# A second seven-product group in every other gate-and-up pair, and silu in one ScalarE pass

## The chip, the cores and the metric

The kernel runs on one core of one Trainium2 chip, in one launch. The metric is the device time of that launch in microseconds, as the median of several runs.

## The reference, cut to what matters

Two layers over 256 tokens of width 2048. Each has a gated mixer (convolution and attention), a SwiGLU feed-forward block with 5632 hidden columns, and an embedding stage. Everything is float32. The part that the change touches is the feed-forward block and the norm ahead of it:

```python
hf = rmsnorm(x, norm_ffn_g[i])
gate, up = jnp.split(hf @ w_gate_up[i], 2, axis=-1)
x = x + (jax.nn.silu(gate) * up) @ w_down[i]
```

## The kernel before, in words

**Splits.** TensorE multiplies in a rounded 32-bit format (`fp32r`). To keep float32's accuracy each operand is split into a high and a low half, and a product is three matmuls: high x high, high x low, low x high (`Sum.add`, lines 175 to 177). A weight tile of 128 x 1024 (two row tiles of 128 by 512 columns; "raw") is fetched by one DMA on SyncE's queue (`fetch`, L134), ScalarE writes its high half `wh` (L140), and VectorE subtracts to get the low half `wl` (L141). There are seven `raw` buffers, and four each of `wh` and `wl`. Activations are split once, when a norm or an `operand` is made, and stay in `pair` buffers, of which there are 23.

**Chunks.** A weight matrix is cut into chunks of 512 output columns. A chunk of w_gate_up has 16 row tiles ("column tiles" of the activation), in four groups of four. In the plain form (`plain`) one raw takes part in 12 matmuls of 128 x 512: two row tiles, two blocks of 128 tokens, three matmuls each.

**The seven-product form.** `fast_chunks` computes two chunks together (w1 and w2; in the feed-forward block a gate chunk and the up chunk that belongs to it). For one group of four row tiles the activation is seen as a 2 x 2 block matrix and the weights as another, and the eight block products are replaced by seven (Winograd's form of Strassen's scheme), named p1, q5, q7, q6, c21, c11 and c12 after the sums that they go to. Each product is six matmuls. The weight sums that it needs are made from the four raws a11, a21, a22, a12 with four 1024-wide adds on VectorE (L242; one of them goes to a buffer `s3`, called "sum" in the profile, the others are in place), and each of the seven operands is split like a raw. Sums p1, q5, q6, q7 stand in the four `ms` banks of PSUM and are combined (L255 on ScalarE; L256, L257 and two L242 on VectorE) as soon as q6 is done. c11, c12, c21, c22 stand in the four `mm` banks; into them go also all plain halves of the other groups. `go` takes the next such half from the list `left`: it fetches, splits and multiplies it, and unless it is called quietly it lets one waiting piece of other work run (`run`). Such pieces are the "turns": transposing the result of the pair before and splitting it into the operand of the next matrix.

**Activations for that form.** An object of `Fast` keeps the blocks of four column tiles and four differences of them (L325), split into high and low halves (L334 on ScalarE, L335 on VectorE). `Norm` makes one such object for its column tiles 0 to 3; the others are split plainly (`halves`, L287 and L288 with the norm's gain, L284 and L285 without). `operand` does the same for the hidden tiles: the first chunk of each part gives a `Fast`, the others plain tiles.

**The feed-forward block.** The 11 pairs c = 0 to 10 run in three parts of 3, 4 and 4. After each part its hidden chunks are multiplied with w_down, two output chunks at a time. Pair c = 0 is computed plainly; all others go through `fast_chunks` with `norm.fast` and the groups that begin at tiles 4, 8 and 12 in the plain form. When the gate chunk is complete, `gate` is called: a Sigmoid with the norm's scale on ScalarE (L868) and a scalar-tensor-tensor on VectorE (L869) give silu; when the up chunk is complete, L877 multiplies.

The order of instructions on each engine is made by the framework's scheduler when the kernel is built: it follows the program's order by priority, but can put an instruction ahead of others when its inputs and a buffer are there. Buffers of a pool are handed out as they come free.

Of the kernel before, what the change touches and what calls it, by code (L numbers as in the profile page):

```python
# [10 lines left out]
F32 = mybir.dt.float32  # L11
# [5 lines left out]
P = 128  # L17
# [27 lines left out]
def trunk(ctx, tc, xT, xR, pT, wI, wF, wC, wA, wOut, wGU, wD, wPG, wPP, vec, bF, gF, out):  # L45
# [86 lines left out]
    def fetch(src):  # L132
        raw = raws.tile([P, 2, 512], F32, tag="raw", name=f"raw{next(uid)}")
        nc.sync.dma_start(raw.rearrange("p k n -> p (k n)"), src)  # L134
        return raw

    def split(raw):
        h = whs.tile([P, 2, 512], F32R, tag="wh", name=f"wh{next(uid)}")
        l = wls.tile([P, 2, 512], F32R, tag="wl", name=f"wl{next(uid)}")
        act.activation(h, raw, AF.Copy)  # L140
        dve.tensor_tensor(l, raw, h.bitcast(F32), op=ALU.subtract)  # L141
        return h, l
# [68 lines left out]
    def fast_chunks(fast, w1, w2, xs, ks, first, to=None):  # L211

        nk = 4 * len(ks)
        p1, q5, q6, q7 = (Sum(2, bank_ms) for _ in range(4))
        c11, c12, c21 = (Sum(2 + nk, bank_mm) for _ in range(3))
        c22 = Sum(nk, bank_mm)
        left = deque()
        for w, sums in ((w1, (c11, c12)), (w2, (c21, c22))):  # L220
            for g, k0 in enumerate(ks):
                for half in range(2):
                    left.append((w[1 + g][:, half * 1024 : (half + 1) * 1024], sums, k0 + 2 * half))

        def go(n=1, quiet=False):
            for _ in range(n):
                if left:
                    src, sums, k0 = left.popleft()
                    parts = split(fetch(src))
                    await_x(xs, (k0, k0 + 1))  # L230
                    plain(sums, xs, k0, parts)
                    fill(CONV // 2 + len(left) % 2)
                    if not quiet:
                        run()

        def product(to, which, raw):
            h, l = split(raw)
            xh, xl = fast(which)
            for kk in range(2):
                to.add(xh(kk), xl(kk), h[:, kk, :], l[:, kk, :])  # L240

        add = lambda o, a, b: dve.tensor_tensor(o, a, b, op=ALU.add)  # L242
        a11, a21 = fetch(w1[0][:, :1024]), fetch(w2[0][:, :1024])
        a22, a12 = fetch(w2[0][:, 1024:]), fetch(w1[0][:, 1024:])
        s3 = raws.tile([P, 2, 512], F32, tag="raw", name=f"sum{next(uid)}")
        product(p1, B11, a11)
        add(s3, a11, a21)
        add(a21, a21, a22)
        product(q5, M1, a21)
        go(quiet=True)  # L250
        product(q7, T3, s3)
        add(a11, a11, a21)
        product(q6, T2, a11)
        u1, u4, u3, u5 = [tmp() for _ in range(4)] if to is None else to
        act.activation(u1, p1.t, AF.Copy)  # L255
        dve.tensor_tensor(u4, u1, q6.t, op=ALU.subtract)  # L256
        dve.tensor_tensor(u3, u4, q7.t, op=ALU.add)  # L257
        add(u4, u4, q5.t)
        add(u5, u3, q5.t)
        go()  # L260
        product(c21, N4X, a22)
        go()
        product(c11, B21, a12)
        go()
        add(a12, a12, a11)
        product(c12, B22, a12)
        while len(left) > 2 * len(ks):
            go()
        add(u1, u1, c11.t)
        add(u4, u4, c12.t)  # L270
        first((u1, u4))
        go(2 * len(ks))
        dve.tensor_tensor(u3, c21.t, u3, op=ALU.subtract)
        dve.tensor_tensor(u5, c22.t, u5, op=ALU.subtract)
        return u3, u5
# [94 lines left out]
    class Norm:  # L370


        def __init__(self, gcol, fast=False):
            self.gcol, self.xs, self.tiles = gcol, {}, {}
            self.fast = Fast() if fast else None
            self.ss = small(8)

        def gain(self, k):
# [8 lines left out]

        def turn(self, n):
            for half, pt in turned(lambda b: xt[:, b, n * 512 : (n + 1) * 512]):
                if n == 0 and self.fast:  # L390
                    self.fast.take(half, pt, [self.gain(2 * half + kk) for kk in range(2)])
                    if half == 1:
                        self.xs.update(enumerate(self.fast.column_tiles()))
                    continue
                o = pair(F32R)
                for kk in range(2):
                    k = 4 * n + 2 * half + kk
                    halves(o[:, kk, :], pt[:, kk, :], self.gain(k))
                    self.tiles[k] = o[:, kk, :]
                    self.xs[k] = by_blocks(self.tiles[k])  # L400
# [62 lines left out]
        take(0)  # L463

    def early():
        norm.fast = Fast()
        for j in range(2):
            norm.fast.take(
                j, xin[0][:, j, :].rearrange("p (k s) -> p k s", k=2), [norm.gain(2 * j + kk) for kk in range(2)]
            )  # L470
        norm.xs.update(enumerate(norm.fast.column_tiles()))

    def rest(q):
        def go():
# [15 lines left out]
    for i in range(L):  # L490
# [71 lines left out]
        def logits():  # L562
            pf = bank_ms()
            lhsT = lambda k: wfc[:, k].rearrange("p a h -> p (a h)")
            for k in range(4, KD):
                pe.matmul(pf[:16, :], lhsT=lhsT(k), rhs=norm.tiles[k], start=(k == 4), stop=False)
            for k, (hi, lo) in enumerate(norm.fast.both()):
# [272 lines left out]
                xc = xt[:, b, n * 512 : (n + 1) * 512]  # L840
                dve.tensor_tensor(xc, xc, acc[b], op=ALU.add)  # L841

        norm = Norm(g_ffn, fast=True)
        def onto_x(norm, n):
            def go(y):
                residual(n, y)
# [3 lines left out]

        for n in range(0, N4, 2):
            onto_x(norm, n + 1)(
                fast_chunks(fast_merged, wOut[i, n], wOut[i, n + 1], merged, (4, 8, 12), onto_x(norm, n))
            )


        after = Norm(g_ple, fast=True)
        c0 = 0
        for part, nch in enumerate(FFN_PARTS):
            hid = {}  # L860
            fast_hid = Fast()
            for c in range(c0, c0 + nch):
                w1, w2 = wGU[i, 2 * c], wGU[i, 2 * c + 1]
                z = [tmp() for _ in range(2)]

                def gate(g, z=z):
                    for b in range(2):
                        act.activation(z[b], g[b], AF.Sigmoid, scale=norm.r(b))  # L868
                        dve.scalar_tensor_tensor(z[b], g[b], norm.r(b), z[b], op0=ALU.mult, op1=ALU.mult)  # L869

                if c == 0:
                    gate(chunk(by_four(w1), norm.xs, bank_mm))
                    up = chunk(by_four(w2), norm.xs, bank_mm)
                else:
                    up = fast_chunks(norm.fast, w1, w2, norm.xs, (4, 8, 12), gate)
                for b in range(2):
                    dve.scalar_tensor_tensor(z[b], up[b], norm.r(b), z[b], op0=ALU.mult, op1=ALU.mult)  # L877
                o = z
                turns.append(
                    lambda c=c, o=o, hid=hid, fast=fast_hid if c == c0 else None:  # L880
                    operand(hid, 4 * c, lambda b: o[b], fast)
                )
            for n in range(0, N4, 2):
                await_x(hid, (4 * c0,))
                on = after if part == len(FFN_PARTS) - 1 else None
                onto_x(on, n + 1)(
                    fast_chunks(
                        fast_hid, wD[i, n][c0 : c0 + nch], wD[i, n + 1][c0 : c0 + nch], hid,
                        range(4 * c0 + 4, 4 * c0 + 4 * nch, 4), onto_x(on, n),
                    )  # L890
                )
# [16 lines left out]
        after = Norm(0 if last else (i + 1) * NV, fast=not last)  # L908
        e = []

        def embedded(n):
# [93 lines left out]
```

## Time and profile before

| what | value |
|---|---|
| median of 3 runs | 2848.05 us (2847.43 to 2848.83) |
| the profiled execution's own time | 2847.62 us |
| its span, first to last instruction | 2845.8 us |
| TensorE busy | 2815.2 us, 99% |
| VectorE busy | 2366.3 us, 83% |
| ScalarE busy | 1556.2 us, 55% |
| mean granted TensorE clock | 0.997 |
| moved by DMA | 543.27 MB, 191 GB/s |

In the profile's rows PE is TensorE, PEld its weight loads, DVE VectorE, ACT ScalarE, SP SyncE, and SPq its DMA queue. A row of a group gives line, engine, operation, output <- inputs, shapes and count; then the busy time in us, the mean of one in ns, and behind the last bar the idle time of the engine just before them with what ended it. A row of a timeline gives start and duration in us, and in square brackets the idle time before it; "x2" means that two in a row are shown as one. A row of the view by stretches gives, for each engine, busy time and instructions in that stretch. A busy TensorE is not one at its peak, since neighbouring matmuls overlap in the rows.

### The profile page before, as it was taken

To read this page: it belongs to the slowest core of one execution; us is meant where nothing else is said; L and a number is where in the kernel's file an instruction comes from. 1 tells how busy PE (TensorE), PEld (TensorE's weight loads), DVE (VectorE), ACT (ScalarE), POOL (GpSimd) and SP (SyncE) were. 2 spreads that over 40 slices of the span, in tenths; PEclk is the share of its full clock that TensorE was granted. 3 is DMA by queue.
4 is the path that set the end of the run, shared out by engine and by line. 5 is a ranking of instruction groups with operands and counts; after the bars stand their busy time and mean duration, and the time that the engine had idled before them with its cause. 6 is when DMAs were issued, how large, how long until landed. Compare 5 with 4: busy or idle time off the path is not lost.

```text
span 2845.8 us, 34651 instructions
## 1 busy us (share of the span) xinstructions
PE 2815.2 (99%) x12724; PEld 2328.0 (82%) x12724; DVE 2366.3 (83%) x3032; ACT 1556.2 (55%) x1874; POOL 9.5 (0%) x40
## 2 busy tenths in 40 slices
PE   8999999999999999999999999999999999999997
PEld 6888888888888888888788888888888888888886
DVE  6998877878888888888869988778688888888886
ACT  6445755555555545556644466455555555455564
POOL 0000000000000000000000000000000000000000
PEclk9999999999999999999999999999999999999999
DMA  7554465565556566555555545555555556556563
GB/s 283 177 179 170 161 205 191 175 205 182 190 199 207 186 203 207 185 193 193 195 174 191 180 155 186 199 192 174 196 193 195 197 196 210 186 195 210 178 217 125
DMA packets 149497, 543.27 MB, mean 191 GB/s; under 512 B 16848, under 2 KB 17104, under 8 KB 149072
## 3 DMA queue, kind: packets, MB, share of 16 engines
q1 hardware_dynamic: 149328, 541.07, 56.0%
q8 instruction: 99, 1.62, 0.2%
q14 instruction: 70, 0.57, 0.1%
HBM read 538.91 MB, written 2.10 MB: 190 GB/s over the span
## 4 chain that ended last, share of the span: by engine, by line
PE 92%; DVE 6%; ACT 1%; issue 1%; DMA 1%; SPq 0%; ACTq 0%; POOLq 0%; POOL 0%; DVEq 0%
PE mm L177 27%; PE mm L176 26%; PE mm L175 26%; PE ms L175 3%; PE ms L177 3%; PE ms L176 3%; DVE wl L141 2%; DVE pair L514 2%; PE ms L297 2%; DMA pair<-in_xT_dram 0%; PE ms L674 0%; ACT wh L140 0%; DVE raw L242 0%; PE ms L710 0%; DMA raw<-in_wI_dram 0%
## 5 line engine op out<-in xcount | busy, mean ns | idle before, releaser
L140 ACT ACTIVATE wh<-raw 128x1024 fp32r<-128x1024 f32 x1110 | 1177.7, 1062 | 1126.2 <-PE mm L177 923.6
L141 DVE TENSOR_TENSOR wl<-raw,wh 128x1024 fp32r<-128x1024 f32 x1110 | 1345.7, 1223 | 424.6 <-ACT wh L140 410.8
L175 PE MATMUL mm<-wh,pair 128*128 128x512 f32 x3552 | 1392.5, 392 | 12.4 <-ACT wh L159 7.5
L176 PE MATMUL mm<-wl,pair 128*128 128x512 f32 x3552 | 1385.6, 390 | 0.5 <-DVE wl L141 0.4
L177 PE MATMUL mm<-wh,pair 128*128 128x512 f32 x3552 | 1385.2, 390 | 0.8 <-DVE pair L285 0.8
L175 PEld LDWEIGHTS mm<-wh,pair 128*128 128x128 f32 x3552 | 667.9, 188 | 148.9 <-ACT wh L159 7.5
L177 PEld LDWEIGHTS mm<-wh,pair 128*128 128x128 f32 x3552 | 667.6, 188 | 141.3 <-DVE pair L285 1.7
L176 PEld LDWEIGHTS mm<-wl,pair 128*128 128x128 f32 x3552 | 668.3, 188 | 138.1 <-DVE wl L141 2.0
L514 DVE SCALAR_TENSOR_TENSOR pair<-pair,vecs,pair 128x256 f32<-128x256 f32 x480 | 203.8, 489 | 0.0
L242 DVE TENSOR_TENSOR raw<-raw,raw 128x1024 f32<-128x1024 f32 x144 | 175.9, 1221 | 1.8
L175 PE MATMUL ms<-wh,pair 128*128 128x512 f32 x416 | 162.9, 392 | 2.1 <-ACT pair L932 2.1
L177 PE MATMUL ms<-wh,pair 128*128 128x512 f32 x416 | 161.9, 389 | 0.0
L176 PE MATMUL ms<-wl,pair 128*128 128x512 f32 x416 | 161.9, 389 | 0.0
L175 PEld LDWEIGHTS ms<-wh,pair 128*128 128x128 f32 x416 | 78.1, 188 | 19.2 <-ACT pair L932 3.2
L177 PEld LDWEIGHTS ms<-wh,pair 128*128 128x128 f32 x416 | 78.1, 188 | 16.3
L176 PEld LDWEIGHTS ms<-wl,pair 128*128 128x128 f32 x416 | 78.1, 188 | 16.0
L140 ACT ACTIVATE wh<-sum 128x1024 fp32r<-128x1024 f32 x48 | 51.0, 1063 | 65.4 <-PE mm L177 65.4
L141 DVE TENSOR_TENSOR wl<-sum,wh 128x1024 fp32r<-128x1024 f32 x48 | 58.6, 1221 | 11.6 <-ACT wh L140 11.6
L242 DVE TENSOR_TENSOR sum<-raw,raw 128x1024 f32<-128x1024 f32 x48 | 58.6, 1221 | 1.5 <-DMA raw<-in_wGU_dram 0.9
L841 DVE TENSOR_TENSOR xt<-xt,tmp 128x512 f32<-128x512 f32 x80 | 51.8, 684 | 0.0
L242 DVE TENSOR_TENSOR tmp<-tmp,mm 128x512 f32<-128x512 f32 x80 | 51.5, 681 | 0.0
L242 DVE TENSOR_TENSOR tmp<-tmp,ms 128x512 f32<-128x512 f32 x80 | 51.2, 681 | 0.0
(176 smaller groups left out, 1142.8 us busy)
## 6 DMA issues: line engine op xcount, KB each, us to landing
raw<-in_wGU_dram SPq DMA_DIRECT2D x352, 512.0 KB, 4.3
raw<-in_wI_dram SPq DMA_DIRECT2D x287, 512.0 KB, 4.0
raw<-in_wD_dram SPq DMA_DIRECT2D x176, 512.0 KB, 4.0
raw<-in_wOut_dram SPq DMA_DIRECT2D x64, 512.0 KB, 3.9
raw<-in_wPG_dram SPq DMA_DIRECT2D x64, 512.0 KB, 4.2
raw<-in_wA_dram SPq DMA_DIRECT2D x32, 512.0 KB, 4.6
raw<-in_wC_dram SPq DMA_DIRECT2D x32, 512.0 KB, 4.7
raw<-in_wPP_dram SPq DMA_DIRECT2D x8, 512.0 KB, 5.1
```

What stands on the lines that cost most here:

```text
L140: act.activation(h, raw, AF.Copy)
L141: dve.tensor_tensor(l, raw, h.bitcast(F32), op=ALU.subtract)
L175: pe.matmul(self.t, lhsT=xh, rhs=wh, start=start, stop=False)
L176: pe.matmul(self.t, lhsT=xh, rhs=wl, start=False, stop=False)
L177: pe.matmul(self.t, lhsT=xl, rhs=wh, start=False, stop=self.left == 0)
L242: add = lambda o, a, b: dve.tensor_tensor(o, a, b, op=ALU.add)
L297: pe.transpose(pt[:, kk * S + b * P : kk * S + (b + 1) * P], src(b)[:, c : c + P], ident)
L514: dve.scalar_tensor_tensor(cv[c], u[c][:, j : j + S], w, cv[c], op0=ALU.mult, op1=ALU.add,)
L841: dve.tensor_tensor(xc, xc, acc[b], op=ALU.add)
```

## The change

`fast_chunks` takes a list of `Fast` objects and does one seven-product group for each. `Norm` can make several; the norm ahead of the feed-forward block now makes two, for column tiles 0 to 3 and 4 to 7. Pairs with odd c (1, 3, 5, 7, 9) use both, and have the groups at 8 and 12 left in the plain form; pairs with even c keep one. With two groups, p1, q5, q6, q7 gather both before they are combined, and `run` is held back until then (`state["quiet"]`). `gate` is a single Silu with the norm's scale on ScalarE. All other callers pass one object.

```diff
-        p1, q5, q6, q7 = (Sum(2, bank_ms) for _ in range(4))
-        c11, c12, c21 = (Sum(2 + nk, bank_mm) for _ in range(3))
+        p1, q5, q6, q7 = (Sum(nf, bank_ms) for _ in range(4))
+        c11, c12, c21 = (Sum(nf + nk, bank_mm) for _ in range(3))
...
+        for g, f in enumerate(fast):
+            a11, a21 = fetch(w1[g][:, :1024]), fetch(w2[g][:, :1024])
+            a22, a12 = fetch(w2[g][:, 1024:]), fetch(w1[g][:, 1024:])
+            s3 = raws.tile([P, 2, 512], F32, tag="raw", name=f"sum{next(uid)}")
+            product(p1, f(B11), a11)
+            add(s3, a11, a21)
+            add(a21, a21, a22)
+            product(q5, f(M1), a21)
             go()
+            product(q7, f(T3), s3)
+            add(a11, a11, a21)
+            product(q6, f(T2), a11)
+            if g == len(fast) - 1:
+                act.activation(u1, p1.t, AF.Copy)
+                dve.tensor_tensor(u4, u1, q6.t, op=ALU.subtract)
+                dve.tensor_tensor(u3, u4, q7.t, op=ALU.add)
+                add(u4, u4, q5.t)
+                add(u5, u3, q5.t)
+                state["quiet"] = False
+                go()
+            product(c21, f(N4X), a22)
+            if len(left) > 2 * len(ks):
+                go()
+            product(c11, f(B21), a12)
+            if g == 0 and len(left) > 2 * len(ks):
+                go()
+            add(a12, a12, a11)
+            product(c12, f(B22), a12)
+        go(len(left) - 2 * len(ks))
...
-            self.fast = Fast() if fast else None
+            self.fast = [Fast() for _ in range(fast)]
...
-                if n == 0 and self.fast:
-                    self.fast.take(half, pt, [self.gain(2 * half + kk) for kk in range(2)])
+                if n < len(self.fast):
+                    self.fast[n].take(half, pt, [self.gain(4 * n + 2 * half + kk) for kk in range(2)])
...
-        norm = Norm(g_ffn, fast=True)
+        norm = Norm(g_ffn, fast=2)
...
-                        act.activation(z[b], g[b], AF.Sigmoid, scale=norm.r(b))
-                        dve.scalar_tensor_tensor(z[b], g[b], norm.r(b), z[b], op0=ALU.mult, op1=ALU.mult)
+                        act.activation(z[b], g[b], AF.Silu, scale=norm.r(b))
...
-                    up = fast_chunks(norm.fast, w1, w2, norm.xs, (4, 8, 12), gate)
+                    nf = 1 + c % 2
+                    up = fast_chunks(norm.fast[:nf], w1, w2, norm.xs, (4, 8, 12)[nf - 1 :], gate)
```

More of the change, by code (lines that the diff above doesn't have):

```diff
@@ L211, in fast_chunks @@
     def fast_chunks(fast, w1, w2, xs, ks, first, to=None):
-        nk = 4 * len(ks)
-        p1, q5, q6, q7 = (Sum(2, bank_ms) for _ in range(4))
-        c11, c12, c21 = (Sum(2 + nk, bank_mm) for _ in range(3))
+        nf, nk = 2 * len(fast), 4 * len(ks)
+        p1, q5, q6, q7 = (Sum(nf, bank_ms) for _ in range(4))
+        c11, c12, c21 = (Sum(nf + nk, bank_mm) for _ in range(3))
         c22 = Sum(nk, bank_mm)
@@ L222, in fast_chunks, with go, product @@
                 for half in range(2):
-                    left.append((w[1 + g][:, half * 1024 : (half + 1) * 1024], sums, k0 + 2 * half))
-        def go(n=1, quiet=False):
+                    left.append((w[len(fast) + g][:, half * 1024 : (half + 1) * 1024], sums, k0 + 2 * half))
+        state = dict(quiet=True)
+        def go(n=1):
             for _ in range(n):
[L227 to L236, printed above, removed]
+                src, sums, k0 = left.popleft()
+                parts = split(fetch(src))
+                await_x(xs, (k0, k0 + 1))
+                plain(sums, xs, k0, parts)
+                fill(CONV // 2 + len(left) % 2)
+                if not state["quiet"]:
+                    run()
+        def product(to, operand, raw):
             h, l = split(raw)
-            xh, xl = fast(which)
+            xh, xl = operand
             for kk in range(2):
@@ L242, in fast_chunks @@
         add = lambda o, a, b: dve.tensor_tensor(o, a, b, op=ALU.add)
[L243 to L253, printed above, removed]
-        u1, u4, u3, u5 = [tmp() for _ in range(4)] if to is None else to
[L255 to L267, printed above, removed]
-            go()
+        u1, u4, u3, u5 = [tmp() for _ in range(4)] if to is None else to
+        for g, f in enumerate(fast):
[6 more added lines that the diff above has]
+            product(q5, f(M1), a21)
+            go()
+            product(q7, f(T3), s3)
[18 more added lines that the diff above has]
+        go(len(left) - 2 * len(ks))
         add(u1, u1, c11.t)
@@ L271, in fast_chunks @@
         first((u1, u4))
-        go(2 * len(ks))
+        go(len(left))
         dve.tensor_tensor(u3, c21.t, u3, op=ALU.subtract)
@@ L370, in trunk, with __init__ @@
     class Norm:
-        def __init__(self, gcol, fast=False):
+        def __init__(self, gcol, fast=0):
             self.gcol, self.xs, self.tiles = gcol, {}, {}
-            self.fast = Fast() if fast else None
+            self.fast = [Fast() for _ in range(fast)]
             self.ss = small(8)
@@ L389, in turn @@
             for half, pt in turned(lambda b: xt[:, b, n * 512 : (n + 1) * 512]):
-                if n == 0 and self.fast:
-                    self.fast.take(half, pt, [self.gain(2 * half + kk) for kk in range(2)])
+                if n < len(self.fast):
+                    self.fast[n].take(half, pt, [self.gain(4 * n + 2 * half + kk) for kk in range(2)])
                     if half == 1:
-                        self.xs.update(enumerate(self.fast.column_tiles()))
+                        self.xs.update(zip(range(4 * n, 4 * n + 4), self.fast[n].column_tiles()))
                     continue
@@ L465, in early @@
     def early():
-        norm.fast = Fast()
+        norm.fast = [Fast()]
         for j in range(2):
-            norm.fast.take(
+            norm.fast[0].take(
                 j, xin[0][:, j, :].rearrange("p (k s) -> p k s", k=2), [norm.gain(2 * j + kk) for kk in range(2)]
             )
-        norm.xs.update(enumerate(norm.fast.column_tiles()))
+        norm.xs.update(enumerate(norm.fast[0].column_tiles()))
     def rest(q):
@@ L566, in logits @@
                 pe.matmul(pf[:16, :], lhsT=lhsT(k), rhs=norm.tiles[k], start=(k == 4), stop=False)
-            for k, (hi, lo) in enumerate(norm.fast.both()):
+            for k, (hi, lo) in enumerate(norm.fast[0].both()):
                 pe.matmul(pf[:16, :S], lhsT=lhsT(k), rhs=hi, start=False, stop=False)
@@ L852, in trunk @@
             onto_x(norm, n + 1)(
-                fast_chunks(fast_merged, wOut[i, n], wOut[i, n + 1], merged, (4, 8, 12), onto_x(norm, n))
+                fast_chunks([fast_merged], wOut[i, n], wOut[i, n + 1], merged, (4, 8, 12), onto_x(norm, n))
             )
-        after = Norm(g_ple, fast=True)
+        after = Norm(g_ple, fast=1)
         c0 = 0
@@ L887, in trunk @@
                     fast_chunks(
-                        fast_hid, wD[i, n][c0 : c0 + nch], wD[i, n + 1][c0 : c0 + nch], hid,
+                        [fast_hid], wD[i, n][c0 : c0 + nch], wD[i, n + 1][c0 : c0 + nch], hid,
                         range(4 * c0 + 4, 4 * c0 + 4 * nch, 4), onto_x(on, n),
@@ L907, in trunk @@
                 nc.sync.dma_start(gb[n], gF[n * 1024 : (n + 1) * 1024].partition_broadcast(P))
-        after = Norm(0 if last else (i + 1) * NV, fast=not last)
+        after = Norm(0 if last else (i + 1) * NV, fast=int(not last))
         e = []
```

## The prediction

> **What bounds the kernel now.** I read the page first (engines, slices), then its groups, the chain that ended last, the waits, and last the timelines of VectorE and TensorE inside the feed-forward stage.
>
> ```profile
> span 2845.8 us, 34651 instructions
> PE 2815.2 (99%) x12724; PEld 2328.0 (82%) x12724; DVE 2366.3 (83%) x3032; ACT 1556.2 (55%) x1874; POOL 9.5 (0%) x40
> PEclk9999999999999999999999999999999999999999
> PE 92%; DVE 6%; ACT 1%; issue 1%; DMA 1%; SPq 0%; ACTq 0%; POOLq 0%; POOL 0%; DVEq 0%
> L140 ACT ACTIVATE wh<-raw 128x1024 fp32r<-128x1024 f32 x1110 | 1177.7, 1062 | 1126.2 <-PE mm L177 923.6
> L141 DVE TENSOR_TENSOR wl<-raw,wh 128x1024 fp32r<-128x1024 f32 x1110 | 1345.7, 1223 | 424.6 <-ACT wh L140 410.8
> L175 PE MATMUL mm<-wh,pair 128*128 128x512 f32 x3552 | 1392.5, 392 | 12.4 <-ACT wh L159 7.5
> ```
>
> TensorE is idle for 2845.8 - 2815.2 = 30.6 us in all, holds 92% of the chain, and its clock is full in every slice. ScalarE's splits wait for TensorE (923.6 us: a `wh` buffer has to come free) and VectorE's wait for ScalarE: both feeders run ahead of TensorE as far as four buffers allow. So a matmul that goes away is time, as long as VectorE can still keep ahead. The next rows are three stretches: the chunk pair c=1, the pair c=2, and the first w_down pair, in layer 0; then matmuls in a steady stretch.
>
> ```profile
> core 0: us, PE busy (x) PEld busy (x) DVE busy (x) ACT busy (x) POOL busy (x), PEclk, DMA share, GB/s
> 656.70:699.80 43.10, 43.10 (x195) 35.74 (x194) 36.92 (x40) 24.56 (x26) 0.00 (x0) 1.00 0.57 195
> 699.80:742.90 43.10, 43.10 (x195) 35.75 (x194) 35.75 (x38) 22.78 (x24) 0.00 (x0) 1.00 0.57 196
> 742.90:775.80 32.90, 32.50 (x147) 26.66 (x146) 30.69 (x34) 17.30 (x18) 0.00 (x0) 1.00 0.54 183
> ```
> ```profile
> 999.86 0.39 PE L175 MATMUL mm<-wh,pair 128*128 128x512 f32 x1
> 1002.58 0.39 PE L175 MATMUL mm<-wh,pair 128*128 128x512 f32 x1
> ```
>
> These two rows are twelve matmuls apart: 2.72 us, 0.2267 us each. The mean of 392 ns in the groups is not the price, since neighbours overlap. A pair has 186 large matmuls, 42.2 us, and eight transposes, 0.8 us: 43.0 of its 43.10. It is bound by TensorE alone, with VectorE at 36 of 43.
>
> The rule of the Trainium skill on this (TensorE: Matmul & The Clock Gate, Back-to-back issue gap) gives some 131 ns for a sustained N=512 matmul; by it the 60 matmuls below would be worth an estimated 7.9 us instead of 13.6. The trace's pitch of 227 ns disagrees, and the sum uses the trace.
>
> **What VectorE does in a pair.** The timeline of VectorE across the fast group of pair c=2:
>
> ```profile
> 698.45 1.22 DVE L141 TENSOR_TENSOR wl<-raw,wh 128x1024 fp32r<-128x1024 f32 x1 [1.49 <-ACT wh L140]
> 700.78 1.41 DVE L877 SCALAR_TENSOR_TENSOR tmp<-tmp,rt,tmp 128x512 f32<-128x512 f32 x2
> 702.11 1.22 DVE L141 TENSOR_TENSOR wl<-sum,wh 128x1024 fp32r<-128x1024 f32 x1
> 703.24 2.36 DVE L141 TENSOR_TENSOR wl<-raw,wh 128x1024 fp32r<-128x1024 f32 x2
> 706.56 2.59 DVE L141 TENSOR_TENSOR wl<-raw,wh 128x1024 fp32r<-128x1024 f32 x2 [0.96 <-ACT wh L140]
> 709.06 0.68 DVE L256 TENSOR_TENSOR tmp<-tmp,ms 128x512 f32<-128x512 f32 x1
> ...
> 712.53 1.28 DVE L242 TENSOR_TENSOR tmp<-tmp,ms 128x512 f32<-128x512 f32 x2
> 713.72 1.28 DVE L285 TENSOR_TENSOR pair<-ms,pair 128x512 fp32r<-128x512 f32 x2
> 714.92 4.72 DVE L141 TENSOR_TENSOR wl<-raw,wh 128x1024 fp32r<-128x1024 f32 x4
> 721.13 2.54 DVE L141 TENSOR_TENSOR wl<-raw,wh 128x1024 fp32r<-128x1024 f32 x2 [1.49 <-ACT wh L140]
> 730.35 1.22 DVE L242 TENSOR_TENSOR sum<-raw,raw 128x1024 f32<-128x1024 f32 x1
> ```
>
> Start to start, back to back, a 1024-wide operation costs 1.14 us (two end after 2.36, of which the last takes 1.22), a 512-wide one 0.60 (two in 713.72 - 712.53), a scalar-tensor-tensor 0.665 (two in 702.11 - 700.78). In the plain part VectorE idles 1.49 us at every split. From the evictions at 709.06 to 721 it does not idle at all: that is the tight place. The row at 730.35 is an add of the next pair, done early in the slack of the plain part: the order on the engine is not the program's.
>
> **The change part by part.**
>
> *Ten more fast groups.* The pairs c=1, 3, 5, 7, 9 of both layers put a second group through seven products. A product is six matmuls: 7 x 6 = 42 in place of 4 x 12 = 48. Saved: 10 x 6 x 0.2267 = 13.6 us of TensorE. Per group VectorE gains three splits and four adds, 7 x 1.14 = 8.0 us, ScalarE three conversions, 3 x 1.06 = 3.2. The bytes fetched stay the same.
>
> *Silu.* It takes two L869 out of every pair: 22 pairs x 2 x 0.665 = 29 us of VectorE; ScalarE keeps two passes. TensorE does not wait there, so it is worth nothing by itself, but it pays for part of the adds.
>
> ```profile
> L869 DVE SCALAR_TENSOR_TENSOR tmp<-tmp,rt,tmp 128x512 f32<-128x512 f32 x40 | 28.2, 746 | 0.0
> L868 ACT ACTIVATE tmp<-tmp,rt 128x512 f32<-128x512 f32 x40 | 26.5, 710 | 0.0
> L803 ACT ACT_TABLE_LOAD x8 | 10.3, 1283 | 0.1
> ```
>
> No row shows a Silu; I give it the Sigmoid's 0.71 us. Its table may have to be loaded once per layer and Sigmoid's loaded again in the embedding stage: four loads of 1283 ns at most. The first of each layer falls into the plain pair c=0, where ScalarE idles 1.66 us per split; the second into the embedding stage, whose feeders have less lead. Bounds 0 and 2 x 1.28 = 2.6 us; I take 0, nearer to ScalarE's 55%. The Trainium skill (ScalarE: Activation LUTs, What ACT_TABLE_LOAD costs) adds a drain of about 1.38 us to the same 1283 ns; by it the upper bound would be an estimated 5.3 us.
>
> *Totals on VectorE.* Odd pair: 14 + 8 splits and 8 adds, 30 x 1.14 = 34.2; eight evictions and combinations 4.8; two L877 1.3; the operand of the pair before (two L285) 1.2: 41.5 us. TensorE in it: 180 x 0.2267 + 0.8 = 41.6. Even pair: 23 x 1.14 + 4.8 + 1.3 + 1.2 = 33.5 against 43.0. So VectorE has 75.0 us of work in the 84.6 us of two pairs: it does not become the bound on the mean, but an odd pair leaves it nothing, and four buffers carry only some microseconds from the even pair over.
>
> *The tight place of an odd pair.* It is now behind q6 of the second group, where the evictions come. Count from the end of q6. TensorE has one plain half (2.72), transposes (0.8), three products (4.08), and then needs the low half of the next plain split after 2.72 + 0.8 + 4.08 + 0.23 = 7.8 us. VectorE has to do by then four evictions (2.4), the splits of c11, c12 and that plain half (3.4), the operand (1.2), and the last add (1.14, unless it was done before): 7.0 to 8.1. Short by at most 0.3: c=5 and c=9 lose 0 to 0.5, taken 0.3. For c=3 and c=7 nothing is pending from the w_down stage: neither operand nor transposes, 5.8 to 7.0 against 7.0: 0. For c=1 the operand is that of c=0, which builds the fast form of the hidden tiles; this case stands in the trace of before:
>
> ```profile
> 670.63 0.75 DVE L325 TENSOR_TENSOR pair<-pair 128x256 f32<-128x256 f32 x2
> 673.11 1.22 DVE L335 TENSOR_TENSOR pair<-pair,pair 128x1024 fp32r<-128x1024 f32 x1
> 676.52 4.62 DVE L141 TENSOR_TENSOR wl<-raw,wh 128x1024 fp32r<-128x1024 f32 x4
> 678.29 0.39 PE L176 MATMUL mm<-wl,pair 128*128 128x512 f32 x1
> ```
>
> Four subtractions (1.4) and two L335 (2.3) stand in place of 1.2, and the split that ends at 676.52 + 1.22 = 677.74 is used at 678.29: 0.55 us to spare with one group. With two, VectorE has 9.4 to 10.6 against 7.8: 1.6 to 2.8 short, taken 2.2. Sum of the shortages: per layer 2.2 + 2 x 0.3, both layers 5.6 us; bounds 3.2 and 8.
>
> *The raw buffers.* Two groups in a row hold four raws and a sum each, out of seven buffers. From 655 to 786 us SyncE waits almost only for a split to release a raw, and a fetch lands 4.0 us after its issue:
>
> ```profile
> SPq L134 <- DVE wl L141: 102.3, 46, 5.9
> DMA to landing us min/median/max: 3.0/4.0/6.0
> ```
>
> The second group's q5 needs its third raw. If that takes the buffer that c21 frees, there lie between a plain half, c11, a plain half, c12 and p1 on TensorE, 2 x 2.72 + 3 x 1.36 = 9.5 us, against 4.0 + 1.22 (add) + 1.06 (conversion) = 6.3: hidden. If it takes the one that c12 frees, the cover is 2.7 us plus the lead. Bounds 0 and 6.3 - 2.7 = 3.6 us per odd pair. I take 0: the first order is that in which buffers come free.
>
> *The norm's second fast group.* In the second w_out pair four L288 (4 x 0.40) give way to four L325 (4 x 0.34) and two L335 (2 x 1.14): VectorE +2.0 us, ScalarE two more 1.06.
>
> ```profile
> 580.00:600.00 20.00, 20.00 (x95) 16.69 (x94) 16.50 (x21) 12.66 (x19) 0.00 (x0) 1.00 0.73 249
> ```
>
> VectorE has 3.5 us free in these 20, and the same build costs TensorE nothing visible at c=1 (43.10 as at c=2). Bounds 0 and 2 x 2.0; taken 1.0 for both layers. The rest of the diff (lists in place of one object, `state`, the counting of `go`) issues the same instructions for all other callers: 0.
>
> **Sum.** -13.6 + 5.6 + 1.0 = -7.0 us. The profiled execution took 2847.6 us, its span and 1.8 around it; the median of the runs is 0.4 higher. 2848.05 - 7.0 = 2841.0.
>
> **The rivals.**
>
> *Full gain.* The order on VectorE puts urgent splits ahead of operand and evictions, as it put a split between the subtractions at c=1 already. Then nothing of the 13.6 us is lost: 2834.5. Against it: 41.5 of 41.6 us leaves no room for any wait.
>
> *VectorE eats it.* Every odd pair loses some 1.4 us in the tight place because adds of the second group could not be done early: 10 x 1.36 = 13.6 comes back, 2848. For it: the w_down pair above, where VectorE works 30.7 of 32.9 us, already shows 0.4 us of TensorE idle. Against it: the first group has free time, TensorE 17.7 us against ten splits, an add and 2.5 us of leftovers, 15.1.
>
> *Slower: the third raw comes late.* By the second order above VectorE stands at an add with splits queued behind it, and TensorE runs dry between the groups. It decides from 1.36 us per odd pair on, less the 0.7 that are lost anyway. With half of the bound, 1.8 us, and the shortages: -7.0 + 18 = +11, 2859; with all 3.6 us it is 2877. For it: SyncE's longest wait of 5.9 us for a raw. Against it: at present seven buffers fetch far ahead, and the adds at 730.35 are made 12 us before their pair begins.
>
> **How the numbers follow.** Forecast 0.50, full gain 0.17, VectorE eats it 0.18, late raw 0.15. The predicted time is the forecast's, 2841.0; its own range is 2837 to 2845 (shortages 3.2 to 8, norm and table 0 to 6). The range for 8 in 10 runs from just below full gain, 2834, to 2853, which takes in the second rival and the milder part of the third. Within 0.2% means 5.7 us, about what a measurement of this kernel tells from no change. The forecast lies 7.0 below, so part of it (0.12) falls within: faster 0.38 + 0.17 + 0.02 = 0.57, same 0.12 + 0.12 + 0.01 = 0.25, slower 0.04 + 0.14 = 0.18.
>
> **What the changed kernel's profile would show.** 60 fewer large matmuls. An odd pair without loss lasts 41.6 to 41.8 us; c=3 and c=7 should be there, c=5 and c=9 within 0.5 of it, c=1 near 44. L869 gone as an operation of VectorE; VectorE's busy time up by 10 x 8.0 - 29 + 4 = 55 us, to about 2421. TensorE's idle time grown by some 7 us, its waits in odd pairs on L141 behind L325 or L335, not on a DMA. The prediction is wrong if pairs of c=3 and c=7 are longer than 42.5 us (raws or adds late), if even pairs grow beyond 43.1 (lead not regained), or if a table load stands in front of a split for which TensorE waits.

## The result, and the profile after

The changed kernel takes 2864.5 us (median of 6 runs, 2861.76 to 2865.61) against 2847.76 us: a ratio of 1.0057, 95% interval [1.0047, 1.0068]. It is slower by 16.7 us, where 7 us less were forecast; the time lies above the range (2834 to 2853 us) and inside what the third rival gives (2859 to 2877 us); whether it does so for that rival's reason, the experiments have to tell.

The page after, its engines, chain and groups:

```profile
span 2859.9 us, 34646 instructions
PE 2816.6 (98%) x12664; PEld 2315.5 (81%) x12664; DVE 2421.0 (85%) x3062; ACT 1585.6 (55%) x1912; POOL 9.5 (0%) x40
PE 86%; DVE 10%; ACT 2%; issue 1%; DMA 1%; SPq 0%; ACTq 0%; POOLq 0%; POOL 0%; DVEq 0%
L140 ACT ACTIVATE wh<-raw 128x1024 fp32r<-128x1024 f32 x1130 | 1189.8, 1060 | 1114.1 <-PE mm L177 768.9
L141 DVE TENSOR_TENSOR wl<-raw,wh 128x1024 fp32r<-128x1024 f32 x1130 | 1363.6, 1221 | 376.1 <-ACT wh L140 363.2
```

The 60 matmuls are gone (12724 to 12664), VectorE's busy time is the 2421 us that was foretold, and still the chain has moved: VectorE holds 10% of it instead of 6%. TensorE's idle time grew by 12.7 us (30.6 to 43.3). Its busy time should have fallen by the 13.6 us of the 60 matmuls and rose by 1.4 instead: a wait that is shorter than the overlap of neighbouring rows counts as busy (c=4 below: 44.29 us busy for 196 matmuls that took 43.10 before), and behind one wait the clock is lower (c=1 below). One wait has grown eightfold. Who waited for whom, before and after (total us, times, longest):

```profile
ACT wh L140 <- DVE raw L242: 22.6, 18, 3.7
```
```profile
ACT wh L140 <- DVE raw L242: 179.4, 64, 5.9
```

ScalarE stands at the conversion of a weight sum that VectorE has not made yet, with the conversions of later halves queued behind it.

*Where the time went.* The pairs c=3 to c=6 of layer 0, each from the last evictions of the pair before (L273, after the change L277) to its own; before, then after. The last row of the second view is a stretch inside c=3 and c=4.

```profile
core 0: us, PE busy (x) PEld busy (x) DVE busy (x) ACT busy (x) POOL busy (x), PEclk, DMA share, GB/s
807.90:849.60 41.70, 41.70 (x186) 34.54 (x185) 34.48 (x36) 21.40 (x23) 0.00 (x0) 1.00 0.63 210
849.60:892.70 43.10, 43.10 (x196) 35.76 (x195) 37.90 (x42) 24.57 (x27) 0.00 (x0) 1.00 0.58 195
892.70:935.80 43.10, 43.10 (x196) 35.76 (x195) 35.75 (x38) 22.78 (x25) 0.00 (x0) 1.00 0.57 195
935.80:978.90 43.10, 43.10 (x196) 35.75 (x195) 35.75 (x39) 22.79 (x25) 0.00 (x0) 1.00 0.56 195
```
```profile
810.90:851.60 40.70, 40.41 (x179) 33.05 (x178) 38.67 (x39) 23.04 (x25) 0.00 (x0) 1.00 0.62 203
851.60:897.20 45.60, 44.29 (x196) 35.52 (x195) 39.03 (x42) 25.07 (x28) 0.00 (x0) 1.00 0.59 197
897.20:939.80 42.60, 42.29 (x190) 34.44 (x189) 40.02 (x41) 24.64 (x27) 0.00 (x0) 1.00 0.55 185
939.80:983.80 44.00, 43.71 (x196) 35.73 (x195) 36.85 (x39) 23.20 (x26) 0.00 (x0) 1.00 0.61 204
836.90:871.70 34.80, 33.94 (x151) 27.17 (x150) 34.12 (x40) 19.20 (x21) 0.00 (x0) 1.00 0.55 182
```

The odd pairs did become shorter, by 1.0 and 0.5 us. The even pair behind each became longer, by 2.5 and 0.9. In the last row VectorE works 34.12 of 34.80 us, from the evictions of c=3 across the boundary to the last sum of c=4. Its timeline there (the lines behind L242 have moved by two to four, so L256 is now L258, L325 L329, L335 L339):

```profile
836.86 0.68 DVE L258 TENSOR_TENSOR tmp<-tmp,ms 128x512 f32<-128x512 f32 x1
837.45 1.22 DVE L242 TENSOR_TENSOR raw<-raw,raw 128x1024 f32<-128x1024 f32 x1
...
843.97 3.49 DVE L141 TENSOR_TENSOR wl<-raw,wh 128x1024 fp32r<-128x1024 f32 x3
847.38 1.22 DVE L242 TENSOR_TENSOR sum<-raw,raw 128x1024 f32<-128x1024 f32 x1
848.63 2.48 DVE L242 TENSOR_TENSOR raw<-raw,raw 128x1024 f32<-128x1024 f32 x2
...
867.04 1.22 DVE L339 TENSOR_TENSOR pair<-pair,pair 128x1024 fp32r<-128x1024 f32 x1
868.17 1.22 DVE L141 TENSOR_TENSOR wl<-raw,wh 128x1024 fp32r<-128x1024 f32 x1
869.31 1.22 DVE L339 TENSOR_TENSOR pair<-pair,pair 128x1024 fp32r<-128x1024 f32 x1
870.44 1.22 DVE L242 TENSOR_TENSOR raw<-raw,raw 128x1024 f32<-128x1024 f32 x1
```

and ScalarE's, which waits three times in this stretch for a sum; these are the last two:

```profile
850.03 2.01 ACT L140 ACTIVATE wh<-raw 128x1024 fp32r<-128x1024 f32 x2 [5.04 <-DVE raw L242]
871.75 2.01 ACT L140 ACTIVATE wh<-raw 128x1024 fp32r<-128x1024 f32 x2 [3.54 <-DVE raw L242]
```

Before, the sums of c=4 were begun 13 us ahead of the pair, which began at 849.6:

```profile
836.71 1.22 DVE L242 TENSOR_TENSOR sum<-raw,raw 128x1024 f32<-128x1024 f32 x1
```

Now they are made from 847 on, just before the pair begins at 851. Over both layers, from the same marks, in us per pair against before (mean of the two layers; c=0 and c=1 together; c=3 of layer 0 is 41.7 before and 40.7 after, of layer 1 42.2 and 41.3):

| pair | c=0, 1 | c=2 | c=3 | c=4 | c=5 | c=6 | c=7 | c=8 | c=9 | c=10 |
|---|---|---|---|---|---|---|---|---|---|---|
| change, us | +3.9 | 0.0 | -0.9 | +2.4 | -0.5 | +0.9 | -0.8 | +2.2 | -0.5 | +0.7 |

c=4 and c=8 lose more than c=6 and c=10. Like c=1, they build the fast form of the hidden tiles (L329 and L339 in the timeline above).

c=1 loses by itself: that form is built in it in the place behind q6 of the second group. VectorE's timeline there, the matmul that waits with the one behind it, and a stretch of 3.6 us from then on:

```profile
687.31 1.22 DVE L141 TENSOR_TENSOR wl<-raw,wh 128x1024 fp32r<-128x1024 f32 x1
688.45 0.42 DVE L329 TENSOR_TENSOR pair<-pair,pair 128x256 f32<-128x256 f32 x1
688.78 1.22 DVE L339 TENSOR_TENSOR pair<-pair,pair 128x1024 fp32r<-128x1024 f32 x1
689.92 0.68 DVE L242 TENSOR_TENSOR tmp<-tmp,mm 128x512 f32<-128x512 f32 x1
690.51 1.22 DVE L339 TENSOR_TENSOR pair<-pair,pair 128x1024 fp32r<-128x1024 f32 x1
691.65 0.68 DVE L242 TENSOR_TENSOR tmp<-tmp,mm 128x512 f32<-128x512 f32 x1
692.25 4.63 DVE L141 TENSOR_TENSOR wl<-raw,wh 128x1024 fp32r<-128x1024 f32 x4
```
```profile
692.94 0.61 PE L175 MATMUL ms<-wh,pair 128*128 128x512 f32 x1 [2.94 <-ACT wh L140]
693.52 0.79 PE L176 MATMUL mm<-wl,pair 128*128 128x512 f32 x1
```
```profile
692.90:696.50 3.60, 3.56 (x8) 2.59 (x9) 3.60 (x4) 0.59 (x1) 0.00 (x0) 0.54 0.19 60
```

The matmul at 692.94 is an early one of the next pair and waits for ScalarE. The one at 693.52 needs the low half that VectorE begins at 692.25 and ends at 693.47, so TensorE would have stood until then in any case. Behind the wait the granted clock is 0.54 for 3.6 us, where the prediction had found it full in every slice: an estimated 3.6 x 0.46 = 1.7 us more. Layer 1 shows the same, a wait of 2.92 us and some 3.4 us at a clock of 0.52.

### The profile page after: what moved, and what is told of

Read it like the earlier page. It is cut to its first block, busy times and chain, and to the rows that moved or that the text cites. A ratio compares the mean times of both kernels' runs of the same rounds, so it can differ in the third digit from the quotient of the medians.

```text
span 2859.9 us, 34646 instructions
## 1 busy us (share of the span) xinstructions
PE 2816.6 (98%) x12664; PEld 2315.5 (81%) x12664; DVE 2421.0 (85%) x3062; ACT 1585.6 (55%) x1912; POOL 9.5 (0%) x40
## 4 chain that ended last, share of the span: by engine, by line
PE 86%; DVE 10%; ACT 2%; issue 1%; DMA 1%; SPq 0%; ACTq 0%; POOLq 0%; POOL 0%; DVEq 0%
PE mm L176 24%; PE mm L177 24%; PE mm L175 24%; DVE wl L141 4%; PE ms L175 4%; PE ms L177 4%; PE ms L176 4%; DVE pair L518 2%; PE ms L301 1%; ACT wh L140 1%; DVE tmp L242 1%; DVE raw L242 1%; DVE pair L339 0%; DMA pair<-in_xT_dram 0%; PE ms L678 0%
## 5 line engine op out<-in xcount | busy, mean ns | idle before, releaser
L141 DVE TENSOR_TENSOR wl<-raw,wh 128x1024 fp32r<-128x1024 f32 x1130 | 1363.6, 1221 | 376.1 <-ACT wh L140 363.2
L175 PE MATMUL mm<-wh,pair 128*128 128x512 f32 x3452 | 1349.9, 393 | 14.3 <-ACT wh L159 7.9
L176 PE MATMUL mm<-wl,pair 128*128 128x512 f32 x3452 | 1351.3, 391 | 3.8 <-DVE wl L141 3.5
L177 PE MATMUL mm<-wh,pair 128*128 128x512 f32 x3452 | 1348.0, 391 | 0.8 <-DVE pair L289 0.8
L175 PEld LDWEIGHTS mm<-wh,pair 128*128 128x128 f32 x3452 | 649.6, 188 | 150.5 <-ACT wh L140 10.6
L176 PEld LDWEIGHTS mm<-wl,pair 128*128 128x128 f32 x3452 | 650.1, 188 | 144.7 <-DVE wl L141 11.6
L177 PEld LDWEIGHTS mm<-wh,pair 128*128 128x128 f32 x3452 | 649.8, 188 | 136.3 <-DVE pair L289 1.7
L242 DVE TENSOR_TENSOR raw<-raw,raw 128x1024 f32<-128x1024 f32 x174 | 212.6, 1222 | 3.2
L175 PE MATMUL ms<-wh,pair 128*128 128x512 f32 x496 | 194.9, 394 | 9.4 <-ACT wh L140 8.5
L176 PE MATMUL ms<-wl,pair 128*128 128x512 f32 x496 | 193.8, 391 | 0.0
L177 PE MATMUL ms<-wh,pair 128*128 128x512 f32 x496 | 193.1, 389 | 0.0
L175 PEld LDWEIGHTS ms<-wh,pair 128*128 128x128 f32 x496 | 93.1, 188 | 33.4 <-ACT wh L140 12.7
L177 PEld LDWEIGHTS ms<-wh,pair 128*128 128x128 f32 x496 | 93.1, 188 | 19.1
L176 PEld LDWEIGHTS ms<-wl,pair 128*128 128x128 f32 x496 | 93.2, 188 | 18.9
L242 DVE TENSOR_TENSOR sum<-raw,raw 128x1024 f32<-128x1024 f32 x58 | 70.9, 1222 | 6.5 <-DMA raw<-in_wGU_dram 5.2
L242 DVE TENSOR_TENSOR tmp<-tmp,mm 128x512 f32<-128x512 f32 x80 | 52.3, 680 | 0.0
L242 DVE TENSOR_TENSOR tmp<-tmp,ms 128x512 f32<-128x512 f32 x80 | 51.2, 681 | 0.3
```

The source lines that it names most:

```text
L175: pe.matmul(self.t, lhsT=xh, rhs=wh, start=start, stop=False)
L176: pe.matmul(self.t, lhsT=xh, rhs=wl, start=False, stop=False)
L177: pe.matmul(self.t, lhsT=xl, rhs=wh, start=False, stop=self.left == 0)
```

## The experiments

**Which part of the change: e1_one_group.** `nf = 1` in place of `nf = 1 + c % 2`; silu and the norm's two objects stay.

> The changed kernel with one seven-product group in every pair (silu and the norm's two fast objects stay). Theory V (the second group's work on VectorE costs the time): everything that was lost comes back and nothing is won, 2847 to 2849 us, pairs of 43.1 us. Rival N (the norm's second object, its extra buffers or the table loads of silu cost it): the loss stays, 2858 to 2865 us.

2848.03 us, ratio 1.0001 [0.9991, 1.0011]; pairs of 43.09 us. Silu with its table loads and the second `Fast` of the norm cost nothing: the second groups cost the 30 us (16.7 lost and 13.6 not won).

**More work on VectorE: e4_no_silu.**

```diff
-    act.activation(z[b], g[b], AF.Silu, scale=norm.r(b))
+    act.activation(z[b], g[b], AF.Sigmoid, scale=norm.r(b))
+    dve.scalar_tensor_tensor(z[b], g[b], norm.r(b), z[b], op0=ALU.mult, op1=ALU.mult)
```

> The changed kernel with Sigmoid and the scalar-tensor-tensor in place of Silu: 1.33 us more on VectorE in each of the 22 pairs. Theory V: it falls into the stretch where VectorE has no idle time, at least in odd pairs, so 10 x 1.33 = 13 us or up to 20 x 1.33 = 27 us more: 2875 to 2892 us. Rival R: VectorE's work does not matter, 2862 to 2867 us.

2880.37 us, ratio 1.0114 [1.0099, 1.0129]: 15.9 us more than with silu. c=4 and c=8 grow by 2.1 us each, c=6 by 1.1, c=5 by nothing: most of the work lands in the even pairs. c=0 and c=1 together grow by 1.6 us, and there the granted clock is at 0.50 for 6.5 us of layer 0. Silu, worth nothing alone, is worth 16 us beside the second groups.

**Less work on VectorE: e5_no_sums.** For the second group `add(a21[:, 0, few], ...)` and its two sisters with `few = slice(0, 8)`, no `s3`.

> The changed kernel with the second group's weight sums left out: three of the four adds cover 8 columns instead of 1024, the one into the buffer of its own is dropped and q7 takes the first raw, so ten pairs give other numbers; products, splits and fetches stay. VectorE has 10 x some 4 us less. Theory V: nearly all of the 13.6 us of TensorE comes out, 2834 to 2845 us, and c4 and c8 fall back to 43.1 us. Rival B (the four PSUM banks of p1, q5, q6, q7 are held through both groups, so the transposes of the pair before come late, whatever VectorE does): 2858 to 2865 us.

2851.97 us, ratio 1.0016 [1.0006, 1.0025]. 12.5 us come back, 7 us fewer than I expected at the least: neither number. The sums are somewhat less than half of the 30 us; the three extra splits and conversions stay. Most of it comes back in c=1 (4.1 us per layer) and in the other odd pairs (0.6 to 0.9 us each). The even pairs do not follow: c=4 and c=8 still take 45.1 us, where I expected 43.1, and c=2 grows to 45.0. So the second group's sums are not what the even pairs pay for by themselves; VectorE still works 33.68 of the 34.0 us from the evictions of c=3 on (836.0 to 870.0). Rival B, the held PSUM banks, falls as the whole cause, since the banks are held as before.

**Raw buffers: e3_raws8.** `RAWS = 8`; `nsel` is one tile of 128 x 128.

> The changed kernel with eight raw buffers in place of seven. Room is made by one selector tile for all eight attention heads, so the forget term of seven heads is not that of the reference; the instructions are the same in number and shape. Rival R: fetches and sums of the second group come earlier, 2836 to 2850 us. Theory V: VectorE has the same work in the same time, 2860 to 2866 us.

2862.51 us, ratio 1.0051 [1.0036, 1.0066], and every pair as after: c=4 45.35, c=6 43.92. An eighth buffer gives back 2 us at most, which is within the noise. And in the changed kernel VectorE's sums wait for a fetched raw for only 5.7 us in all, in six waits. The late raw, my third rival, is not the cause.

**The sums on another engine: e2_pool_adds.** `add` of the second group by `nc.gpsimd.tensor_tensor`.

> The changed kernel with the four weight sums of the second group made by GpSimd, which is idle. Theory V: VectorE is relieved of 10 x 4 x 1.14 = 46 us, the odd pair falls from 41.5 to 36.9 us of its work, so most of the 13.6 us saved on TensorE shows: 2833 to 2842 us, and c4 and c8 go back to about 43.1 us. Rival R (the raw buffers and late fetches cost it): GpSimd's slower adds hold the raws longer, 2864 us or more.

2888.14 us, ratio 1.0142 [1.0127, 1.0157], 24 us slower still. The time is what rival R gave, and the expectation of theory V fails. The trace shows on which premise: VectorE was not relieved, its busy time grew from 2421.0 to 2442.1 us. Its groups, and a stretch of its and GpSimd's timelines:

```profile
L141 DVE TENSOR_TENSOR wl<-raw,wh 128x1024 fp32r<-128x1024 f32 x1130 | 1427.6, 1278 | 378.9 <-ACT wh L140 365.4
L243 POOL TENSOR_TENSOR raw<-raw,raw 128x1024 f32<-128x1024 f32 x30 | 90.5, 3015 | 90.9 <-DVE wl L141 90.1
```
```profile
825.50 11.21 DVE L141 TENSOR_TENSOR wl<-raw,wh 128x1024 fp32r<-128x1024 f32 x4
836.64 1.21 DVE L141 TENSOR_TENSOR wl<-sum,wh 128x1024 fp32r<-128x1024 f32 x1
```
```profile
824.43 3.26 POOL L243 TENSOR_TENSOR sum<-raw,raw 128x1024 f32<-128x1024 f32 x1 [134.84 <-DVE raw L243]
827.76 3.26 POOL L243 TENSOR_TENSOR raw<-raw,raw 128x1024 f32<-128x1024 f32 x1
832.24 3.39 POOL L243 TENSOR_TENSOR raw<-raw,raw 128x1024 f32<-128x1024 f32 x1 [1.21 <-DVE wl L141]
```

Four splits take 11.21 us where they took 4.7, with three GpSimd adds beside them. The splits as a whole grew by 1427.6 - 1363.6 = 64 us, more than the 40 adds that left VectorE (49 us). The Trainium skill (SBUF — State Buffer, Who interferes with whom) states that a VectorE instruction with two inputs in SBUF contends with a GpSimd instruction that reads SBUF. The trace agrees: the three adds take 3.3 to 3.4 us each and lie beside the splits for 8.8 us, and the four splits take 6.5 us more. ScalarE also waits 92.6 us in all for GpSimd's sums themselves, so this run does not separate VectorE's longer work from sums that come late.

**The same instructions in another order: e6_spread_odd.** Two more plain halves between the second group's last products, taken from the tail of the pair:

```diff
-            if len(left) > 2 * len(ks):
+            if len(left) > 2 * len(ks) or g == 1:
                 go()
             product(c11, f(B21), a12)
-            if g == 0 and len(left) > 2 * len(ks):
+            if g == 1 or len(left) > 2 * len(ks):
                 go()
```

> The changed kernel with the same instructions in another order in odd pairs: two more plain halves between the second group's last three products, so the tight place behind q6 has 5.4 us more of TensorE's work as cover and the tail of the pair one half instead of three. If it is the burst behind q6 that costs (theory V, burst): c1 falls by 2 to 4 us and the sum to 2845 to 2856 us. If VectorE's work over the whole stretch from the odd pair to the even pair's evictions is the limit (theory V, stretch), the wait moves to the even pairs: 2858 to 2866 us.

2864.04 us, ratio 1.0058 [1.0043, 1.0073]: no change of the sum, but the wait moves. c=0 and c=1 together fall from 91.3 to 86.7 us, c=2 rises from 43.1 to 48.6 (49.2 in layer 1), and c=5 falls by 1.1 while c=6 rises by 1.0; c=4 stays at 45.4. Part of the rise of c=2 is again the clock: in layer 0 it is at 0.57 for four us behind a wait of 3.7 us. The burst behind q6 alone is not what costs; the stretch is.

**And in even pairs too: e7_spread_all.** `if spread: go()` behind `product(p1, ...)` and behind `product(q7, ...)`, with `spread` in gate-and-up pairs of one group.

> As the run before, and in even pairs two more plain halves between the first four products, so their evictions come 5.4 us later on TensorE. Theory V, stretch: the stretch gets 5.4 us more of cover per pair of pairs, c4 and c8 fall by 1 to 2 us each, sum 2842 to 2856 us. If only the burst behind q6 mattered, no more than the run before. If the raw buffers are too few for plain halves between the sums, slower than the run before.

2844.99 us, ratio 0.9988 [0.9979, 0.9998]: 19.5 us less than the changed kernel, with as many instructions on TensorE, VectorE and ScalarE (12664, 3062, 1912). The stretches c=3 to c=6 in layer 0:

```profile
813.00:854.20 41.20, 41.20 (x184) 34.11 (x183) 38.60 (x39) 24.07 (x25) 0.00 (x0) 1.00 0.62 211
854.20:897.00 42.80, 42.80 (x194) 35.40 (x193) 38.77 (x43) 24.93 (x28) 0.00 (x0) 1.00 0.61 200
897.00:939.30 42.30, 42.30 (x193) 35.07 (x192) 39.88 (x41) 24.88 (x27) 0.00 (x0) 1.00 0.58 191
939.30:981.80 42.50, 42.50 (x193) 35.27 (x192) 36.47 (x39) 23.30 (x26) 0.00 (x0) 1.00 0.61 206
```

TensorE is busy throughout, and c=5 with c=6 takes 84.8 us in place of 86.2: 1.4 less, the 1.36 of one group in full. c=2 still loses, more than c=0 and c=1 now gain (0.8 us): it takes 48.4 us in layer 0 and 45.8 in layer 1. With only one plain half left behind the products of c=1, the sums of c=2 are made behind the evictions of c=1, and TensorE waits 2.28 us for the high half of one of them, in both layers alike. The difference is the clock: 0.51 for 6.7 us behind that wait in layer 0 (first row), full throughout c=2 in layer 1 (second row).

```profile
706.00:712.70 6.70, 6.54 (x15) 4.82 (x16) 5.84 (x6) 3.85 (x4) 0.00 (x0) 0.51 0.53 162
2110.20:2156.00 45.80, 43.07 (x193) 35.20 (x192) 39.02 (x40) 23.82 (x26) 0.00 (x0) 1.00 0.59 195
```

**The lead itself: e11_tmps7 and e12_five_halves.** The first frees room (seven `tmps`, one `nsel` tile); the second also has `pool("whs", 5)` and `pool("wls", 5)`.

> Control for the run after it: the changed kernel with seven tmp buffers in place of nine and one selector tile for all attention heads (the forget term of seven heads is not that of the reference). If the tmp buffers don't matter: 2861 to 2866 us.

> As the control, with five buffers each for the high and the low halves of the weights in place of four. If VectorE's free time in the plain tail of even pairs is lost because the halves can't be kept (lead of four buffers), a fifth gives up to one plain half, 2.7 us, of lead ahead of each stretch: 20 us less at most over ten stretches, I expect 8 to 18 us less than the control. If the lead does not matter because VectorE falls behind whatever it starts with, or the weight sums that ScalarE waits for set the pace: within 3 us of the control.

The control takes 2863.18 us (ratio 1.0053 [1.0038, 1.0068]), the second 2845.15 us (0.9990 [0.9980, 0.9999]): 18.0 us less, with order and instructions of the source unchanged. Its c=3 to c=6:

```profile
810.20:851.50 41.30, 41.30 (x184) 34.17 (x183) 38.74 (x40) 23.92 (x26) 0.00 (x0) 1.00 0.56 190
851.50:895.40 43.90, 43.35 (x193) 35.17 (x192) 38.65 (x42) 24.42 (x28) 0.00 (x0) 1.00 0.63 216
895.40:937.00 41.60, 41.60 (x189) 34.51 (x188) 39.09 (x41) 24.09 (x26) 0.00 (x0) 1.00 0.52 177
937.00:980.90 43.90, 43.90 (x196) 35.78 (x195) 37.51 (x40) 23.32 (x27) 0.00 (x0) 1.00 0.61 216
```

The odd pair c=5 has the 41.6 us that I foretold for one without loss. Not all of the 18.0 us is lead for the stretch, though. Of the 15.7 us between the two profiled executions 13.0 lie in the feed-forward blocks and 3.8 in the embedding stage, which the change does not touch (before the first block the control is 1.0 us quicker). Within the blocks c=0 and c=1 together gain 3.5 us per layer and c=2 gives back 2.2; c=4 and c=8 gain 1.4 each, c=5 and c=9 1.1, while c=6 and c=10 stay as they were (43.95 us). ScalarE waits even longer for the sums (219.3 us against 179.0 in the control); with a buffer more, less of it reaches TensorE.

**Towards a faster kernel.** e8_c0_fast sends c=0 through `fast_chunks` too, with one group in all pairs.

> One group per pair as before the change, with silu and one fast object in the norm, but pair c=0 through the seven-product form too. VectorE has room there, so 2 x 6 matmuls x 0.2267 = 2.7 us less: 2844 to 2846 us if theory V holds (a group costs nothing where VectorE is idle); 2848 to 2852 us if the transposes of the norm's last columns, which fall into that pair, hold it up.

2844.87 us, ratio 0.9990 [0.9980, 1.0000], 3 us less than e1_one_group: in c=0, where VectorE worked only 27.5 of 43.0 us before, a group gives what its matmuls cost. e9_four_and_c0 joins this with the order of e7_spread_all and leaves c=1 out: `nf = 2 if c in (3, 5, 7, 9) else 1`.

> Second group only in the pairs c=3, 5, 7, 9; the plain halves spread between the products in all pairs with one group; c=0 through the seven-product form. Theory V, stretch: each of the eight groups gives its 1.36 us once VectorE has cover, 10.9 us, and c=0 in both layers 2.7 us: 2848 - 13.6 = 2834 us, 2832 to 2838 us. If the gains are eaten elsewhere (c=0 hands a shorter lead to c=1, which builds the fast hidden tiles): 2838 to 2848 us.

2836.67 us, ratio 0.9964 [0.9950, 0.9978]: the fastest of all, 11 us under the kernel before. Its page:

```profile
span 2834.3 us, 34618 instructions
PE 2803.2 (99%) x12664; PEld 2314.2 (82%) x12664; DVE 2425.9 (86%) x3078; ACT 1591.0 (56%) x1914; POOL 9.5 (0%) x40
```

It has as many matmuls as the changed kernel and more VectorE work, and is 28 us faster. e10_five_and_c0 adds a second group in c=2, `c in (2, 3, 5, 7, 9)`, and spreads the halves in the first w_down pairs.

> The run before, and a second group in c=2 too, with the plain halves spread in the first w_down pairs that follow. VectorE then has two stretches of two groups in a row (c=2 and c=3 with only the w_down pairs between, in which it works 30.7 of 32.9 us). Theory V, stretch: c=2 gains at most 1.36 us and the w_down pair after it loses 1 to 3 us: 2833 to 2840 us, not faster than the run before. If only the building of the fast hidden tiles makes a second group dear: 2831 to 2833 us.

2844.53 us, ratio 0.9987 [0.9978, 0.9997]. In layer 0 c=2 falls from 43.1 to 42.6 us and the first w_down pair rises from 32.9 to 35.4. Not faster, as the stretch had it, but 4.5 us above what I expected at the most. Of the 7.6 us between the two profiled executions 4.5 lie in the feed-forward blocks, 1.9 ahead of the first of them, and 1.3 in the embedding stage, where this execution has four us at a clock of 0.57 and the other has none.

## Why the prediction was wrong

- **Matmuls saved, 13.6 us**: right in kind and size. e7_spread_all gives 1.4 us for the one group in c=5 with c=6, e8_c0_fast 3 us for two groups.
- **Silu, table loads, the norm's second object** (0, 0 to 2.6, 1.0): right within 1 us; e1_one_group shows 0 for all of them together. Silu takes 0.71 us, and four table loads of 1283 ns were added, two at L872 and two at the embedding's Sigmoid.
- **The shortages in the tight place, 5.6 us**: the right place, mis-sized. From the table, with 1.36 us as the gain of each group: c=1 lost 5.3 us (taken 2.2), c=3 and c=7 together 1.0 (taken 0), c=5 and c=9 1.7 (taken 0.6): 16 us for both layers. The working left out two things. The evictions of c11 and c12 (L242 at 689.92 and 691.65 in c=1) stand ahead of the urgent split at 692.25 and are 1.2 us more for VectorE there. And behind the wait in c=1 the clock is down, an estimated 1.7 us, where the working counted every matmul at 227 ns.
- **The step that failed** is the one behind "Totals on VectorE": 75.0 of 84.6 us, so the even pair pays the odd one's debt. I gave every odd pair a full lead, looked only inside odd pairs, and gave the even ones 0. They lost 12 us over both layers (c=4 +2.4, c=6 +0.9, c=8 +2.2, c=10 +0.7). For c=4 and c=8 the total itself was too small: the prediction saw the fast form of the hidden tiles in c=1 alone and counted 1.2 us of operand in every even pair, but c=4 and c=8 build it too, 3.7 us. The sign that the prediction gave for a lost lead, even pairs beyond 43.1 us, is what came. The free time that the mean counts lies in the plain tail of even pairs, where four buffers are full and VectorE may not run ahead; the odd pair's tail, with three plain halves instead of six, is too short to make the next pair's sums early. So from the evictions of the odd pair to the last sum of the even one it is a single full stretch, 34.12 of 34.80 us. e7_spread_all (more of TensorE's work within the stretch, -19.5 us) and e12_five_halves (more lead ahead of it, some 13 us of its -18.0 in the feed-forward blocks) bear it out from both sides. The prediction named the limit, "four buffers carry only some microseconds", and then did not count with it.
- **The rivals.** "VectorE eats it" was the right mechanism with too small a bound: I let it take back the gain, not more. The late raw has the measured time in its span, but that is chance: e3_raws8 and the short waits for fetched raws show that it is not the cause.

What stays open: why the even pairs keep their loss when the second group's sums are left out (e5_no_sums), and why c=6 and c=10 gain nothing from a fifth buffer. And a wait of the same 2.28 us is followed by a lower clock in one layer of e7_spread_all and not in the other; what decides that, no run here shows.

## What to carry to other kernels

A feeding engine with a tenth of its time free on the mean can still be the bound: its work has to be added up over the stretch between two places where it has time to spare, and set against the other engine's work in that stretch plus what the buffers between them hold. When work is moved to such a feeder, the debt shows one stage later, so the stage after the changed one has to be costed too. Before giving up an idea that overloads a stretch, spread the cheap work of the bound engine into it, or deepen the buffer: here they gave 19.5 and 18.0 us, more than the 13.6 us that the change saves on TensorE. Even so both ended only 3 us below the kernel before; it took e9_four_and_c0, which leaves the second group out of c=1, the dearest place, and puts one into c=0, to come 11 us below it.

## What the runs showed of the hardware that was not expected

The idle GpSimd was no free helper here for two-input VectorE work: its 1024-wide in-place add took 3.0 us on the mean, and the splits on VectorE grew by 64 us in sum (11.21 us for four in place of 4.7).

A short wait of TensorE can cost more than itself. In c=1 of the changed kernel a wait of 2.9 us is followed in both layers by some 3.5 us at a granted clock of 0.52 to 0.54, in which the matmuls follow each other at 0.43 us instead of 0.227. The mean clock of that execution, 0.997, is the same as before the change and does not show it.
